# Norm in two steps between products, spread mixes, single-half tiles between full ones, and own bank and buffers at the end of a hybrid decoder step

## The chip, the cores and the metric

The kernel runs on one core of one Trainium2 chip. The metric is the device time of an execution in microseconds (us). TensorE (PE) multiplies, and its weight loads (PEld) overlap with that; VectorE (DVE) and ScalarE (ACT) do the elementwise work; SyncE (SP) issues DMAs in the order of its queue. The program is scheduled when it is built: each engine then has a fixed order of instructions, and semaphores hold an instruction until what it reads is there and what it overwrites is free.

## The reference, cut to what matters

One layer of a decoder for 1024 prompt rows and 8 sample rows (1032 in all, model width 1024). After sparse attention and a gated delta branch, merged by gates into `y`:

```python
x = x + merged @ w_out
hn = rms_norm(x, norm_ffn)
gg, uu = jnp.split(hn @ w_gate_up, 2, axis=-1)     # 1024 x (2 x 2816)
x = x + (jax.nn.silu(gg) * uu) @ w_down            # 2816 x 1024
```

The change touches only this last part: the product with `w_out`, the norm, the gate and up products, and the product with `w_down`.

## The kernel before, in words

Everything is held transposed: 128 model columns on partitions, the 1032 rows along the free axis. The rows form two halves of 516 (`HALF`), each of two quarters of 258 (`QT`). Every float32 factor is split into a high part (ACT, a copy in a rounded type, L187) and a low part (DVE, a difference, L188), and a product is three matmuls per 128 x 128 block: high by high, high by low, low by high (L163 to L165, L1706 to L1708).

`w45` is the last stage. `w_out(s)` makes the eight tiles of x for half s: per tile two products of 24 matmuls with 258 columns into the two buffers of `pj`, an evacuation of each on DVE (L1593, it adds the residual), a square on ACT and a running sum of squares `rs` on DVE (L1595, L1597).

`prepare(s)` is a generator that `w45` advances between other work. It multiplies the squares with ones on PE (L1608), takes the reciprocal root on DVE in ten tiny instructions (`nv`, `nr`, `nt`, L1610 and L196 to L200), transposes the result so that it lies along the free axis (L1616, PE), copies it to SBUF (L1617, ACT), and scales the eight tiles in place on DVE (L1620). Then it splits the blocks B11, B12, B21, B22 of the half, and the sums T1 to T4 of them (L1625), into high and low parts: tiles `hb` (and `b12`) with 1032 columns. For half 0 this runs beside `w_out(1)`, for half 1 beside the first gate and up tiles.

Gate and up have 22 tiles of 128 columns each. The plain form, `gate_up_plain`, does half 0 of the tiles 0 to 2 (`EARLY`), 192 matmuls each, while half 1 isn't ready; `e` counts gate and up in it, and `sg` holds the result. The other form, `gate_up`, is a seven-product scheme of Strassen's kind on quarters: differences of weight blocks are made on DVE (`mix`, L1683, into the scratch tile `rs`), and each of the seven products has 12 matmuls per half, 84 for one half and 168 for both. Its operands lie in seven buffers with the names `whi`, `wlo` and `wx`. The sums stand in four accumulator banks A, B, D, F, two buffers each. D takes the product with T1 first; DVE reads that to make `E` (L1729), then the product with B22 is added into the same bank, and DVE adds the result to `U`. After the plain tiles the single-half tiles 0 to 2 (half 1) come one after another, then tiles 3 to 20 for both halves, then tile 21 as two single halves. Weights come through two buffers `wraw` (L1678, L1679).

`down` multiplies with `w_down` in four groups of tiles. `load_act` reads an activation tile back from memory into a raw buffer (L1748) and splits it into `act`. The first and the second of these share one raw buffer, the start of `rs`. Results go out through `store_y`: transposes on PE (L1788), a copy to `yo` on ACT (L1790, two buffers for all three shapes in turn), and a DMA (L1792, L1794).

Of the kernel before, what the change touches and what calls it, by code (L numbers as in the profile page):

```python
# [9 lines left out]
F32 = mybir.dt.float32  # L10
# [10 lines left out]
T = 1032  # L21
# [33 lines left out]
class K:  # L55
# [1459 lines left out]
    def w45(self):  # L1515
        nc, I, O = self.nc, self.I, self.O
        op, end_o = self.pool("oa", side="right")
        xp, end_x = self.pool("x2")
        yp, end_y = self.pool("y")
        wk, end_wk = self.pool("stage")  # L1520
        rs = self.stage[:, 0:T]
        self.x2h.append(xp.tile([128, 4, T], F32, name="x21", bufs=1))
        x2 = lambda m: self.x2h[m // 4][:, m % 4]
        oa = self.oa = [[op.tile([128, T], F32R, name=f"oa{j}{x}", bufs=1) for x in range(2)] for j in range(4)]
        yhi = yp.tile([128, 8, T], F32R, name="yhi")
        ylo = yp.tile([128, 8, T], F32R, name="ylo")
        self.load_oa(oa, wk, 0, 3)
        weave(self.merge_a(oa, wk, yhi, ylo, 0, 2), PVS, self.sample, 4)
        for _ in self.merge_a(oa, wk, yhi, ylo, 2, 3):
            pass  # L1530
        self.x_T(1)
        end_wk()
        end_o()
        self.end_sa()
        self.nrm = xp
        h0, end_h0 = self.pool("h0", side="right")
        gf = xp.tile([128, 8], F32, name="gf")
        nc.sync.dma_start(gf, I['norm_ffn'][0].rearrange("(k p) -> p k", p=128))
        b12, end_b12 = self.pool("b12", side="right")
        H = [{}, {}]  # L1540
        for _ in self.w_out(0, (yhi, ylo), x2):
            pass
        prep = self.prepare(0, h0, H[0], gf, x2, b12)
        for m, _ in enumerate(self.w_out(1, (yhi, ylo), x2)):
            if m:
                next(prep, None)
        end_y()
        ex, end_ex = self.pool("gx")
        h1, end_h1 = self.pool("h1")
        self.end_pf()  # L1550
        self.end_ps()
        self.ps, end_ps = self.pool("psg", space=PSUM)
        self.pproj = lambda: self.ps.tile([128, 512], F32, name="A", tag="A", bufs=2)
        prep = self.prepare(1, h1, H[1], gf, x2)
        for f in range(EARLY):
            self.gate_up_plain(f, H[0], ex)
            for _ in islice(prep, 2 if f else 1):
                pass
        for _ in prep:
            pass  # L1560
        del self.pproj
        end_b12()
        self.wx, end_wx = self.pool("wx", side="right")
        for f in range(EARLY):
            self.gate_up(f, (1,), H, ex)
        for f in range(EARLY, 21):
            self.gate_up(f, (0, 1), H, ex)
            if f < EARLY + 4:
                nc.sync.dma_start(x2(f - EARLY), self.d_x2[f - EARLY])
        ops = self.gate_up(21, (1,), H, ex)  # L1570
        end_h1()
        a0, end_a0 = self.pool("act0")
        raws = [self.stage[:, 0:T], self.stage[:, 0:T], a0.tile([128, T], F32, name="araw", tag="araw", bufs=2)]
        first = [self.load_act(f, a0, 6, raws[f]) for f in range(3)]
        self.gate_up(21, (0,), H, ex, ops)
        end_ps()
        end_wx()
        end_h0()
        self.down(x2, a0, first)
        end_a0()  # L1580
        end_ex()
        end_x()
# [18 lines left out]
    def prepare(self, s, pool, H, gf, x2, b12=None):  # L1601

        nc = self.nc
        n = 86
        sqa = self.stage[:, HALF * (1 + s):HALF * (2 + s)]
        p = self.pproj()
        for j in range(6):
            nc.tensor.matmul(p[:n, j:j + 1], sqa[:, n * j:n * j + n], self.ones[:, 0:1], start=True, stop=True)  # L1608
        v, r, t = (self.nrm.tile([128, 6], F32, name=x, tag=x, bufs=1)[:n] for x in ("nv", "nr", "nt"))
        nc.vector.tensor_scalar(v, p[:n, 0:6], 1.0 / 1024, EPS, op0=ALU.mult, op1=ALU.add)  # L1610
        self.rsqrt(r, v, t=t)
        for c in range(2):
            p = self.pproj()
            for j in range(3):
                i = 3 * c + j
                nc.tensor.transpose(p[:, n * j:n * j + n], r[:, i:i + 1].to_broadcast([n, 128]), self.ident[:n, :n])  # L1616
            nc.scalar.activation(sqa[:, QT * c:QT * c + QT], p[:, 0:QT], AF.Copy)  # L1617
        for m in range(8):
            xv = x2(m)[:, HALF * s:HALF * s + HALF]
            nc.vector.scalar_tensor_tensor(xv, xv, gf[:, m:m + 1], sqa, op0=ALU.mult, op1=ALU.mult)  # L1620
        yield
        B11, B12, B21, B22 = (self.quarter(s, x) for x in ("B11", "B12", "B21", "B22"))

        def sub(name, dst, a, b):
            nc.vector.tensor_tensor(dst, a, b, op=ALU.subtract)  # L1625
            H[name] = self.block(pool, dst)
        H["B21"] = self.block(pool, B21)
        H["B11"] = self.block(pool, B11)
        yield
        if b12:  # L1630
            H["B12"] = self.block(b12, B12, "b12")
        H["B22"] = self.block(pool, B22)
        yield
        sub("T1", B11, B12, B11)
        sub("T3", B12, B22, B12)
        yield
        sub("T2", B22, B22, B11)
        sub("T4", B21, B21, B22)
        yield
# [9 lines left out]
        self.split(t[:, 0], t[:, 1], src)  # L1649
        return t  # L1650

    def gate_up_plain(self, f, H, ex):

        nc, gu = self.nc, self.I['w_gate_up'][0]
        sg = ex.tile([128, HALF], F32, name="sg", tag="sg", bufs=2)
        ws = [self.wcols(gu, 128 * f), self.wcols(gu, 2816 + 128 * f)]
        for e, (wh, wl) in enumerate(ws):
            for c in range(2):
                tag = "ABDF"[2 * e + c]
                p = self.ps.tile([128, 512], F32, name=tag, tag=tag, bufs=2)[:, :QT]  # L1660
                x1, x2 = H[f"B1{c + 1}"], H[f"B2{c + 1}"]
                self.mm3(p, [(wh[:, k], wl[:, k], x[:, 0, k % 4], x[:, 1, k % 4])
                             for k in range(8) for x in ((x1, x2)[k // 4],)])
                v = sg[:, QT * c:QT * c + QT]
                if e == 0:
                    nc.scalar.activation(v, p, AF.Silu)
                else:
                    nc.vector.tensor_tensor(v, v, p, op=ALU.mult)
        nc.sync.dma_start(self.d_act[f, :, 0:HALF], sg)

    def gate_up(self, f, halves, H, ex, ops=None):

# [21 lines left out]
            return t  # L1694
        U = {}
        st = self.x2h[1][:, 2 * (f % 2):2 * (f % 2) + 2]
        ps = {(t, s): self.ps.tile([128, 512], F32, name=t, tag=t, bufs=2)[:, :QT] for s in halves for t in "ABDF"}

        def product(src, x, t, first):
            a = operand(src)  # L1700
            made.append(a)
            for s in halves:
                b, p = H[s][x], ps[t, s]
                for k in range(4):
                    lh, ll, rh, rl = a[:, k], a[:, 4 + k], b[:, 0, k], b[:, 1, k]
                    nc.tensor.matmul(p, lh, rh, start=(first and k == 0), stop=False, skip_group_check=True)  # L1706
                    nc.tensor.matmul(p, lh, rl, start=False, stop=False, skip_group_check=True)  # L1707
                    nc.tensor.matmul(p, ll, rh, start=False, stop=(k == 3), skip_group_check=True)  # L1708
# [17 lines left out]
        for s in halves:  # L1726
# [1 line left out]
            e = part("E")  # L1728
            nc.vector.tensor_tensor(e, U[s], ps["D", s], op=ALU.add)  # L1729
            add(1, s, 1, e, ps["F", s])  # L1730
        product(lambda: mix(S[3], A12, S[2]), "B22", "D", False)
        for s in halves:
            add(0, s, 1, U[s], ps["D", s])
        product(lambda: A22, "T4", "F", False)
        for s in halves:
            t = slice(HALF * s, HALF * s + HALF)
# [43 lines left out]
    def store_y(self, m, x2, wk):  # L1780
        nc, O = self.nc, self.O
        cs = slice(128 * m, 128 * m + 128)
        for q in range(3):
            i0, ni, n = 4 * q, (4, 4, 1)[q], (128, 128, 8)[q]
            p = self.ptr()
            for j in range(ni):
                r0 = 128 * (i0 + j)
                nc.tensor.transpose(p[:n, j, :], x2(m)[:, r0:r0 + n], self.ident)  # L1788
            y = wk.tile([128, 4, 128], F32, name="yo", tag="yo", bufs=2)
            nc.scalar.activation(y[:n, :ni], p[:n, :ni], AF.Copy)  # L1790
            if q < 2:
                nc.sync.dma_start(O['y_p'][0, 512 * q:512 * q + 512, cs].rearrange("(i p) c -> p i c", p=128), y)  # L1792
            else:
                nc.sync.dma_start(O['y_s'][:, 0, cs], y[:8, 0])  # L1794
# [37 lines left out]
```

## Time and profile before

| what | value |
| --- | --- |
| median of three runs | 1805.31 us (1805.31, 1805.31, 1814.39) |
| profiled execution, its own time | 1802.74 us |
| span of its trace | 1801.0 us |
| PE busy | 1740.0 us, 97% of the span |
| weight loads busy | 1662.6 us |
| DVE busy | 1210.6 us, 67% |
| ACT busy | 852.1 us, 47% |
| mean granted clock | 0.995 |

The span runs from the first to the last instruction of the trace; the execution's own time is 1.7 us longer. Times in the rows are counted from the start of the span. A busy PE is not PE at its peak: matmuls overlap, so the number of matmuls in a stretch says more than its busy share. The stage of the change begins at about 1000 us and lasts to the end.

### The profile page before, as it was taken

The numbers are of one execution on the slowest core, as the hardware profiler recorded it, in microseconds if no ns is written. First come the engines' busy times: TensorE is split into PE (matmuls) and PEld (weight loads), VectorE is DVE, ScalarE is ACT, GpSimd is POOL, SyncE is SP. The second block draws the span as 40 slices with busy tenths as digits, with TensorE's granted clock in tenths as the row PEclk, the third lists the DMA queues.
The fourth block names the chain that finished last, engine by engine and source line by source line (L and its number), as shares of the span: only waits on it lengthen the run. The fifth ranks groups of instructions, "written<-read, shape, count | busy, mean of one in ns | idle before, by whom it ended". The sixth has DMA issues, their size and how long they took to land.

```text
span 1801.0 us, 31724 instructions
## 1 busy us (share of the span) xinstructions
PE 1740.0 (97%) x12276; PEld 1662.6 (92%) x12276; DVE 1210.6 (67%) x2776; ACT 852.1 (47%) x1575; POOL 42.2 (2%) x68
## 2 busy tenths in 40 slices
PE   5998999999999999999999999999999999999998
PEld 5998989999999988878899998999999999999998
DVE  7775558999899777797656477766666665733222
ACT  4567467877845345687444243433333333412012
POOL 3001100000000000000000000000000000000000
PEclk9999999999999999999999999999999999999999
DMA  6115434434546543254567434322222323732122
GB/s 194 43 35 153 130 101 145 130 113 120 159 131 167 149 137 109 84 183 141 195 235 226 138 110 135 101 81 85 82 72 75 91 72 125 223 100 73 51 80 69
DMA packets 293595, 218.01 MB, mean 121 GB/s; under 512 B 39292, under 2 KB 267456, under 8 KB 292412
## 3 DMA queue, kind: packets, MB, share of 16 engines
q1 hardware_dynamic: 291716, 205.50, 37.8%
q0 software_dynamic: 1728, 10.49, 1.7%
q8 instruction: 96, 1.57, 0.4%
q14 instruction: 55, 0.45, 0.1%
HBM read 154.17 MB, written 61.87 MB: 120 GB/s over the span
## 4 chain that ended last, share of the span: by engine, by line
PE 83%; DMA 7%; DVE 5%; ACT 3%; issue 2%; SPq 0%; ACTq 0%; DVEq 0%
PE pj L163 15%; PE pj L165 15%; PE pj L164 15%; PE A L1706 2%; PE A L1707 2%; PE A L1708 2%; PE D L1706 2%; PE F L1706 2%; PE F L1707 2%; PE D L1707 2%; PE F L1708 2%; PE D L1708 2%; PE PT L1055 1%; DMA araw<-d_act 1%; PE B L1706 1%
## 5 line engine op out<-in xcount | busy, mean ns | idle before, releaser
L163 PE MATMUL pj<-xhi,whi 128*128 128x344 f32 x912 | 297.5, 326 | 5.3 <-ACT gs L862 4.3
L165 PE MATMUL pj<-xhi,wlo 128*128 128x344 f32 x912 | 294.3, 323 | 0.0
L164 PE MATMUL pj<-xlo,whi 128*128 128x344 f32 x912 | 293.3, 322 | 0.0
L187 ACT ACTIVATE whi<-wraw 128x1024 fp32r<-128x1024 f32 (+4 forms) x126 | 115.2, 914 | 249.4 <-PE pj L164 208.0
L163 PEld LDWEIGHTS pj<-xhi,whi 128*128 128x128 f32 x912 | 171.9, 189 | 9.3 <-ACT gs L862 5.7
L164 PEld LDWEIGHTS pj<-xlo,whi 128*128 128x128 f32 x912 | 171.9, 188 | 2.0 <-issue 1.1
L165 PEld LDWEIGHTS pj<-xhi,wlo 128*128 128x128 f32 x912 | 171.9, 188 | 1.4
L164 PE MATMUL pj<-act,whi 128*128 128x344 f32 x528 | 170.3, 323 | 0.7 <-DVE act L188 0.7
L165 PE MATMUL pj<-act,wlo 128*128 128x344 f32 x528 | 168.9, 320 | 0.8 <-DVE wlo L188 0.8
L163 PE MATMUL pj<-act,whi 128*128 128x344 f32 x528 | 169.3, 322 | 0.2 <-DVE x L1768 0.2
L188 DVE TENSOR_TENSOR wlo<-wraw,whi 128x1024 fp32r<-128x1024 f32 (+3 forms) x104 | 116.2, 1118 | 54.4 <-ACT whi L187 52.7
L1768 DVE TENSOR_TENSOR x<-pj,x 128x344 f32<-128x344 f32 x96 | 48.5, 514 | 140.0 <-PE pj L165 139.9
L768 DVE TENSOR_SCALAR_CACHE_REDUCE kvb<-S,cand 128x384 bf16<-128x384 f32 (+3 forms) x128 | 103.7, 810 | 2.0
L165 PEld LDWEIGHTS pj<-act,wlo 128*128 128x128 f32 x528 | 99.2, 188 | 1.5 <-DVE wlo L188 1.3
L164 PEld LDWEIGHTS pj<-act,whi 128*128 128x128 f32 x528 | 99.2, 188 | 1.0 <-DVE act L188 1.0
L163 PEld LDWEIGHTS pj<-act,whi 128*128 128x128 f32 x528 | 99.2, 188 | 0.9 <-issue 0.4
L1706 PE MATMUL D<-hb,wx 128*128 128x258 f32 x328 | 93.0, 284 | 2.0 <-DVE E L1729 2.0
L1708 PE MATMUL D<-hb,wx 128*128 128x258 f32 x328 | 92.7, 282 | 0.7 <-DVE wx L188 0.7
L1706 PE MATMUL A<-hb,wlo 128*128 128x258 f32 x328 | 93.0, 283 | 0.0
L1707 PE MATMUL A<-hb,wlo 128*128 128x258 f32 x328 | 92.8, 283 | 0.0
L1708 PE MATMUL A<-hb,wlo 128*128 128x258 f32 x328 | 92.8, 283 | 0.0
L1707 PE MATMUL D<-hb,wx 128*128 128x258 f32 x328 | 92.6, 282 | 0.0
(587 smaller groups left out, 4790.3 us busy)
## 6 DMA issues: line engine op xcount, KB each, us to landing
wraw<-in_w_gate_up SPq DMA_DIRECT2D x50, 512.0 KB
wraw<-in_w_in SPq DMA_DIRECT2D x38, 512.0 KB
d_act<-x SPq DMA_DIRECT2D x41, 258.0 KB
araw<-d_act SPq DMA_DIRECT2D x20, 516.0 KB
d_g<-gs SPq DMA_DIRECT2D x48, 172.0 KB
wraw<-in_w_out SPq DMA_DIRECT2D x16, 512.0 KB
wraw<-in_w_branch SPq DMA_DIRECT2D x12, 512.0 KB
wraw<-in_w_down SPq DMA_DIRECT2D x16, 384.0 KB
```

Of the source, the lines that this page charges most:

```text
L163: nc.tensor.matmul(ps, lh, rh, start=(j == 0), stop=False)
L164: nc.tensor.matmul(ps, lh, rl, start=False, stop=False)
L165: nc.tensor.matmul(ps, ll, rh, start=False, stop=(j == last))
L187: self.nc.scalar.activation(hi, src, AF.Copy)
L188: self.nc.vector.tensor_tensor(lo, src, hi.bitcast(F32), op=ALU.subtract)
L768: nc.vector.tensor_scalar(junk[:r, :n], s, thr[:r, j:j + 1], 0.0, op0=ALU.is_lt, op1=ALU.add, accum_out=cnt[:r, j:j + 1])
L1055: nc.tensor.transpose(p[:, j, :], P[j][:, 128 * s:128 * s + 128], self.ident)
L1706: nc.tensor.matmul(p, lh, rh, start=(first and k == 0), stop=False, skip_group_check=True)
L1707: nc.tensor.matmul(p, lh, rl, start=False, stop=False, skip_group_check=True)
L1708: nc.tensor.matmul(p, ll, rh, start=False, stop=(k == 3), skip_group_check=True)
L1768: nc.vector.tensor_tensor(xv, p, xv, op=ALU.add)
```

## The change

- `prepare` yields once more, between the reciprocal root and the transposes.
- `gate_up_plain` is a generator too and yields after gate and after up; `prepare` for half 1 is advanced one step at each of these six points, where before it took two steps after tile 0, one after each of the tiles 1 and 2, and the rest at once.
- The single-half tiles 0, 1 and 2 come after the full tiles 3, 4 and 5, one each.
- In a `gate_up` for one half, the product with B22 goes into a second buffer of bank B, starts a sum of its own, and is added to `E` (which holds U + D) in place of `U`.
- `sg` is one tile with two halves, and the raw buffer of the second activation is this tile.
- The tiles `yo` for 4 and for 1 block have two buffers each.

```diff
@@ w45
-        for f in range(EARLY):
-            self.gate_up_plain(f, H[0], ex)
-            for _ in islice(prep, 2 if f else 1):
-                pass
-        for _ in prep:
-            pass
+        sg = ex.tile([128, 2, HALF], F32, name="sg", bufs=1)
+        for f in range(EARLY):
+            for _ in self.gate_up_plain(f, H[0], sg[:, f % 2]):
+                next(prep, None)
...
-        for f in range(EARLY):
-            self.gate_up(f, (1,), H, ex)
         for f in range(EARLY, 21):
             self.gate_up(f, (0, 1), H, ex)
+            if f < 2 * EARLY:
+                self.gate_up(f - EARLY, (1,), H, ex)
             if f < EARLY + 4:
                 nc.sync.dma_start(x2(f - EARLY), self.d_x2[f - EARLY])
...
-        raws = [self.stage[:, 0:T], self.stage[:, 0:T], a0.tile([128, T], F32, name="araw", tag="araw", bufs=2)]
+        raws = [self.stage[:, 0:T], sg.rearrange("p a b -> p (a b)"), a0.tile([128, T], F32, name="araw", tag="araw", bufs=2)]
@@ prepare
         self.rsqrt(r, v, t=t)
+        yield
         for c in range(2):
@@ gate_up_plain
-        nc.sync.dma_start(self.d_act[f, :, 0:HALF], sg)
+            if e == 1:
+                nc.sync.dma_start(self.d_act[f, :, 0:HALF], sg)
+            yield
@@ gate_up
+        one = len(halves) == 1
+        bank = lambda t: self.ps.tile([128, 512], F32, name=t, tag=t, bufs=2)[:, :QT]
...
-        product(lambda: mix(S[3], A12, S[2]), "B22", "D", False)
+        if one:
+            ps["D", s], U2 = bank("B"), e
+        product(lambda: mix(S[3], A12, S[2]), "B22", "D", one)
         for s in halves:
-            add(0, s, 1, U[s], ps["D", s])
+            add(0, s, 1, U2 if one else U[s], ps["D", s])
@@ store_y
-            y = wk.tile([128, 4, 128], F32, name="yo", tag="yo", bufs=2)
+            y = wk.tile([128, ni, 128], F32, name="yo", tag=f"yo{ni}", bufs=2)
```

How this moves instructions is seen in the order of the engines. First the first norm, beside `w_out(1)`. On DVE before, from the end of the reciprocal root on (`x_10114` and `x_10241` are the two tiles that hold x):

```order
L200 SCALAR_TENSOR_TENSOR nr<-nt,nr 86x6
L1620 SCALAR_TENSOR_TENSOR x_10114<-x_10114,gf,rs 128x516 x4
L1620 SCALAR_TENSOR_TENSOR x_10241<-x_10241,gf,rs 128x516 x4
L188 TENSOR_TENSOR b_11684<-x_10114,b_11684 128x1032
L1593 SCALAR_TENSOR_TENSOR x_10114<-pj,x_10114 128x258
L188 TENSOR_TENSOR hb<-x_10241,hb 128x1032
L1593 SCALAR_TENSOR_TENSOR x_10114<-pj,x_10114 128x258
```

and in the changed kernel:

```order
L200 SCALAR_TENSOR_TENSOR nr<-nt,nr 86x6
L1591 SCALAR_TENSOR_TENSOR x_10114<-pj,x_10114 128x258
L188 TENSOR_TENSOR wlo<-wraw,whi 128x1024
L1619 SCALAR_TENSOR_TENSOR x_10114<-x_10114,gf,rs 128x516 x4
L1619 SCALAR_TENSOR_TENSOR x_10241<-x_10241,gf,rs 128x516 x4
L1595 TENSOR_TENSOR rs<-rs 128x516
L1591 SCALAR_TENSOR_TENSOR x_10114<-pj,x_10114 128x258 x2
L188 TENSOR_TENSOR b_11745<-x_10114,b_11745 128x1032
```

The evacuations of the two products that were pulled ahead (L1591 here; the first of them a few rows further up) now stand before the scaling (L1619), together with a weight split; the next two come after the scaling and a sum of squares. On PE the two products, 48 matmuls, stand between the sums and the transposes. On ACT before:

```order
L1595 ACTIVATE rs<-x_10114 128x516
L187 ACTIVATE whi<-wraw 128x1024
L1595 ACTIVATE rs<-x_10114 128x516
L1617 ACTIVATE rs<-pj 128x258 x2
L187 ACTIVATE b_11684<-x_10114 128x1032
```

and now:

```order
L187 ACTIVATE whi<-wraw 128x1024
L1593 ACTIVATE rs<-x_10114 128x516
L187 ACTIVATE whi<-wraw 128x1024
L1616 ACTIVATE rs<-pj 128x258 x2
L1593 ACTIVATE rs<-x_10114 128x516
L187 ACTIVATE b_11745<-x_10114 128x1032
```

A weight split (`whi`) and the square of one of the products have moved to the two sides of the norm's copies. The second norm, beside the plain tiles: PE before, around the sums, and further on around the transposes, which stand 53 matmuls later:

```order
L165 MATMUL F<-hb,wlo 128x258
L1608 MATMUL A<-ones,rs 86x1 x6
L163 MATMUL B<-b_11684,whi 128x258
...
L164 MATMUL F<-b_11684,whi 128x258
L1616 MATMUL A<-ident,nr 128x86 x6
L165 MATMUL F<-b_11684,wlo 128x258
```

and now, where the sums stand after the gate half of tile 0, and the transposes 56 matmuls later:

```order
L165 MATMUL B<-hb,wlo 128x258
L1606 MATMUL A<-ones,rs 86x1 x6
L163 MATMUL D<-hb,whi 128x258
...
L164 MATMUL B<-b_11745,whi 128x258
L1615 MATMUL A<-ident,nr 128x86 x6
L165 MATMUL B<-b_11745,wlo 128x258
```

The sums have moved ahead by 48 matmuls, from behind the up half (F) of tile 0 to ahead of it (D, F), and with them the transposes. Last, the DMA queue: before, the second activation was read into `rs` among the last tiles,

```order
L1748 DMA araw<-d_act 128x1032 x2
L1740 DMA d_act<-x_10241 128x516
L1748 DMA rs<-d_act 128x1032
L139 DMA wraw<-in_w_down 128x3x128
L1748 DMA araw<-d_act 128x1032
```

and now it is read into `sg` among the weight loads behind the second single-half tile:

```order
L1744 DMA d_act<-x_10241 128x516
L1679 DMA wraw<-in_w_gate_up 128x8x128
L1752 DMA sg<-d_act 128x1032
L1678 DMA wraw<-in_w_gate_up 128x8x128
L1744 DMA d_act<-x_10241 128x516 x2
```

The load has moved ahead by some fifteen tiles.

## Rows read from the trace of the kernel before

**Rows 1.** Stretches: PE, PEld, DVE, ACT, POOL busy us (count), granted clock, DMA share, GB/s
```profile
1031.00:1040.00 9.00, 5.19 (x36) 5.11 (x36) 7.07 (x20) 2.59 (x5) 0.00 (x0) 0.81 0.27 88
...
1094.00:1150.00 56.00, 49.16 (x370) 46.51 (x369) 47.36 (x74) 26.20 (x43) 0.00 (x0) 0.97 0.42 132
...
1126.00:1136.00 10.00, 8.72 (x71) 8.30 (x69) 7.97 (x15) 4.47 (x9) 0.00 (x0) 1.00 0.34 97
...
1200.00:1500.00 300.00, 300.00 (x2499) 300.00 (x2498) 186.76 (x341) 102.90 (x195) 0.00 (x0) 1.00 0.26 79
```

**Rows 2.** PE's waits from 1000 us on: us in total, times, longest
```profile
PE pj L1616 <- DVE nr L200: 3.8, 1, 3.8
...
PE B L1706 <- ACT whi L187: 3.4, 2, 2.2
...
PE D L1706 <- DVE E L1729: 2.0, 2, 1.0
...
PE pj L165 <- DVE wlo L188: 0.8, 2, 0.5
...
PE pj L164 <- DVE act L188: 0.7, 1, 0.7
```

**Rows 3.** Timeline of PE at the first norm: start, us, what, [idle before <- releaser]
```profile
1030.65 1.01 PE L1608 MATMUL pj<-ones,rs 128*86 128x1 f32 x12
...
1035.46 0.66 PE L1616 MATMUL pj<-ident,nr 86*128 86x86 f32 x6 [3.81 <-DVE nr L200]
...
1036.19 0.42 PE L164 MATMUL pj<-ylo,whi 128*128 128x258 f32 x1
...
1039.42 0.30 PE L164 MATMUL pj<-ylo,whi 128*128 128x258 f32 x1
```

**Rows 4.** Timeline of DVE at the first norm
```profile
1031.87 1.23 DVE L188 TENSOR_TENSOR wlo<-wraw,whi 128x1024 fp32r<-128x1024 f32 x1
...
1033.08 0.68 DVE L1597 TENSOR_TENSOR rs<-rs 128x516 f32<-128x516 f32 x1
...
1036.63 5.42 DVE L1620 SCALAR_TENSOR_TENSOR x<-x,gf,rs 128x516 f32<-128x516 f32 x8 [1.22 <-ACT rs L1617]
...
1041.97 1.23 DVE L188 TENSOR_TENSOR b<-x,b 128x1032 fp32r<-128x1032 f32 x1
...
1043.12 0.42 DVE L1593 SCALAR_TENSOR_TENSOR x<-pj,x 128x258 f32<-128x258 f32 x1
```

**Rows 5.** Timeline of ACT: first norm, end of gate and up, last output
```profile
1024.98 1.06 ACT L187 ACTIVATE whi<-wraw 128x1024 fp32r<-128x1024 f32 x1 [4.15 <-PE pj L164]
...
1035.94 0.66 ACT L1617 ACTIVATE rs<-pj 128x258 f32<-128x258 f32 x2 [3.58 <-PE pj L1616]
...
1534.36 1.07 ACT L187 ACTIVATE act<-rs 128x1032 fp32r<-128x1032 f32 x1 [2.68 <-DMA rs<-d_act]
...
1798.28 0.27 ACT L1790 ACTIVATE yo<-tp 8x128 f32<-8x128 f32 x1 [1.75 <-DMA out_y_p<-yo]
```

**Rows 6.** Timeline of DVE: second norm, last block, a steady tile
```profile
1072.29 0.43 DVE L1593 SCALAR_TENSOR_TENSOR x<-pj,x 128x258 f32<-128x258 f32 x1 [2.23 <-PE pj L165]
...
1084.68 0.16 DVE L1610 TENSOR_SCALAR nv<-A 86x6 f32<-86x6 f32 x1 [0.35 <-PE A L1608]
...
1092.11 5.42 DVE L1620 SCALAR_TENSOR_TENSOR x<-x,gf,rs 128x516 f32<-128x516 f32 x8 [4.23 <-ACT rs L1617]
...
1121.07 1.22 DVE L188 TENSOR_TENSOR hb<-x,hb 128x1032 fp32r<-128x1032 f32 x1
...
1320.18 1.29 DVE L1683 TENSOR_TENSOR rs<-wraw 128x512 f32<-128x512 f32 x2 [0.65 <-DMA wraw<-in_w_gate_up]
```

**Rows 7.** Timeline of the DMA queue: a weight load, the last outputs
```profile
1315.84 0.38 SPq L1679 DMA_DIRECT2D wraw<-in_w_gate_up  x1
...
1795.84 1.09 SPq L1792 DMA_DIRECT2D out_y_p<-yo  x2
...
1798.57 0.30 SPq L1794 DMA_DIRECT2D out_y_s<-yo  x1
```

More of the change, by code (lines that the diff above doesn't have):

```diff
@@ L1650, in block, with gate_up_plain @@
         return t
-    def gate_up_plain(self, f, H, ex):
+    def gate_up_plain(self, f, H, sg):
         nc, gu = self.nc, self.I['w_gate_up'][0]
-        sg = ex.tile([128, HALF], F32, name="sg", tag="sg", bufs=2)
         ws = [self.wcols(gu, 128 * f), self.wcols(gu, 2816 + 128 * f)]
@@ L1696, in gate_up @@
         st = self.x2h[1][:, 2 * (f % 2):2 * (f % 2) + 2]
-        ps = {(t, s): self.ps.tile([128, 512], F32, name=t, tag=t, bufs=2)[:, :QT] for s in halves for t in "ABDF"}
+        one = len(halves) == 1
+        bank = lambda t: self.ps.tile([128, 512], F32, name=t, tag=t, bufs=2)[:, :QT]
+        ps = {(t, s): bank(t) for s in halves for t in "ABDF"}
         def product(src, x, t, first):
```

## Prediction

> **What bounds the kernel now.** I read the stretches of the run first, then PE's waits, then the timelines of PE, VectorE (DVE), ScalarE (ACT) and the DMA queue (SP) where PE waits. In the steady part of the gate and up products PE is busy all the time: 2499 matmuls in 300 us, 0.120 us each, at full granted clock, with DVE at 186.76 of 300 us [rows 1]. There nothing but fewer matmuls would help, and the change leaves the matmul count as it is. What it can win is the time in which PE stands or runs slowly, and that lies in four places.
>
> First norm (1031 to 1040). PE does the small matmuls of the sum, waits 3.81 us for DVE's reciprocal root, does six transposes, and then runs slowly: 15 matmuls from 1036.19 to 1039.42, 0.215 us apart [rows 3]. That is the lower of the two levels of the clock (1.2 GHz), after the long wait. 15 x (0.215 - 0.120) = 1.4 us; with the wait 5.2 us.
>
> Second norm, its blocks, and the three single-half tiles (1094 to 1150). PE does 370 matmuls where 56 us at the steady rate hold 466.5 [rows 1]. The 96.5 missing ones are 11.6 us. The waits name what is late: weights split by ACT 3.4 us, E on DVE about 1 of its 2.0 us, the rest in pieces [rows 2]; the clock's mean falls to 0.97 [rows 1].
>
> End of gate and up, start of down: 1.0 us for E, 0.7 for the second activation, 0.8 for weights, together 2.5 us [rows 2]. The very end: the last small output waits 1.75 us in ACT for an earlier store of the same buffer [rows 5].
>
> **First norm, in two steps.** The transposes move behind two whole products of w_out (48 matmuls, 5.8 us). The root comes 3.8 us after the sums, so this wait and its slow stretch go: -5.2 us. What is new stands in the order. On ACT a weight split (1.06 us) now stands ahead of the two copies of the norm (0.66 us together) [rows 5]; it waits for the same product as the transposes. Let t be the end of that product. Transposes are done at about t + 0.7 (the second group needs DVE's evacuation of that product, 0.43), the first copy at t + 1.4, and only then is the buffer of the next product free: PE stands 0.7 to 0.8 us. On DVE the low part of that weight (1.23) and the eight scalings (5.42) stand ahead of the evacuations; in a row each starts about 0.1 before the one ahead ends [rows 4]: scalings end at t + 1.1 + 1.1 + 5.4 = t + 7.6, the sum of squares takes 0.6, so the first evacuation ends at t + 8.5. The two products after the transposes end at t + 1.4 + 5.8 = t + 7.2, and the third needs that buffer: 1.3 us. New waits 2.1 us; the rest of w_out I walked through the same way, and there each evacuation comes 0.5 us or more ahead of its need. Bounds: 0, if copies and evacuations slip through, and 5.2, if the waits take all back. I take 2.1, since each piece has its row. Net -3.1.
>
> **Second norm, spread mixes, full tile first.** Count from the last evacuation of w_out at 1072.29 [rows 6], where PE starts the plain tiles. Before: the sums reach DVE at +12.4, because the norm begins after a whole plain tile; the scaling starts at +19.8, after 4.23 us of idle DVE, because the transposes stand 53 matmuls behind the sums; then DVE works with hardly a break until the last block is split at +50.0 [rows 6]. PE needs the plain tiles' 288 matmuls and the norm, 35.6 us, and then takes a single tile, of 12 matmuls (1.44 us) a product: the fifth product wants block T2 at +41.4, the last wants T4 at +44.2. Both are earlier than DVE can be. After: sums follow 48 matmuls (+5.8), transposes follow 56 more (+12.9), copies and a weight split 1.8 us, so the scaling starts at +14.7. With the same 30.2 us of DVE work behind it the last block is there at +44.9. The first tile is now a full one, 24 matmuls a product: T2 of the second half is wanted at 35.6 + 9 x 1.44 = +48.6, T4 at +54.3. Cover on both, 4 us or more.
>
> Then the singles. A full tile costs DVE 12.5 us (186.76/300 of 20.2 us). The operands, four differences and seven low parts at about 0.65 us [rows 6], are 7.1 of it and the same for a single; the additions halve. So a single asks 9.8 us of DVE for 10.1 us of PE, and a weight load of 4.34 us from issue (1315.84) to use (1320.18) [rows 6, 7] must fit between its last reader and the next tile. Three in a row leave nothing for it. With full ones between, a pair has 30.2 us of PE for 22.3 us of DVE. The own bank takes away the wait of the B22 product for E; it costs no matmul, since the partial sum is added from SBUF by the addition that stood there anyway. The four reloads of x2 and the stores of the plain tiles stay ahead of the first single's weights in SP; the first single now has a full tile's 20 us as cover. Of 11.6 us I keep 1.0, for a load that is late in the second or third pair, where I find the E additions only about 1 us ahead of PE. Bounds of what stays: 0, and 4.8 (in each of the three the wait of rows 2's second size, 3.4 - 2.2 = 1.2, and the small ones of 0.4). Net -10.6.
>
> **Own buffer for the second activation; own bank in tile 21.** Its load waited in the DMA queue for the split of the first one; ACT then waited 2.68 us for it [rows 5]. Now it is loaded into sg many tiles ahead. With the own bank, 1.0 + 0.7 go; of the 0.8 us for weights, behind a chain of loads that now starts earlier, I count half. Net -2.1, bounds 0 and -2.5.
>
> **Own buffer for the 8-row output.** ACT's last copy waits for a store; without it its DMA follows the previous issue, which ends at 1796.93, in place of 1798.57 [rows 7]. It landed 2.43 us after issue, which gives 1799.4 in place of 1801.0: -1.6, bounds 0 and -1.75.
>
> **Sum.** -3.1 - 10.6 - 2.1 - 1.6 = -17.4 us on the profiled 1802.74, 1785.3. The median of the runs shown, 1805.31, is 2.6 us above the profiled execution, so I forecast 1788 us.
>
> Now the clock, where a rule speaks against the change. After the wait of 3.81 us PE ran at the lower level; in the stretch 1126 to 1136, with PE idle for 1.28 us in all, the granted clock stayed at 1.00 [rows 1 to 3]. The Trainium skill, TensorE: Matmul & The Clock Gate, section "A second HAM failure mode: psum-queue depth-cycling", says that short idle spells between groups of matmuls, from cycling through accumulator banks, can make the clock swing between its levels. The rows side against it for waits near 1 us.
>
> **Rivals.**
> - Clock swings. Each of the two new waits in w_out is followed by a slow stretch like the one in rows 3: 2 x 1.4 = 2.8 us given back, 1791. That is what the rule just named would make of it.
> - The singles still wait: 4.8 us stay in place of 1.0, 1792. For: DVE takes its work in order, and the differences stand behind loads. Against: the pair's cover of 8 us.
> - w_out's evacuations behind DVE's block work cost all that the first norm gave (3.1 less gain), and the singles keep 4.8 (3.8 less): 1795. For: DVE has almost no idle from the scaling to the last block in w_out.
> - The change doesn't do what it says: the waits move from the first single to the first full tile, since DVE's 30 us of work are the same, and only the two last items win, 3.7 us: 1802.
> - Slower: after the two waits in w_out the clock doesn't come back before w_out ends. At 0.095 us a matmul the gain is gone after 17.4/0.095 = 183 matmuls, and 10 products are 240, 22.8 us: 1811. Against: it came back after 15 matmuls [rows 3].
>
> **How the numbers follow.** Forecast (1785 to 1791) 0.57, clock swings 0.08, singles wait 0.16, both evacuations and singles 0.10, waits only moved 0.06, slower 0.03. Half a per cent, 9 us, is about what a measurement can tell from no change. Below 1796.3 lie the first three and about half of the fourth: 0.85. Within: 0.12. Above 1814.3: 0.03, where the lower clock lasts into the plain tiles (278 matmuls or more). The range takes the bounds of all terms towards the fast side (-5.2 - 11.6 - 2.5 - 1.75 = -21.1, 1784; 3 us below that for what the walk leaves out) and reaches over the third rival, to 1798.
>
> **What would show it.** PE's wait of 3.8 us before the transposes is gone, and two of about 0.8 and 1.3 us stand in w_out, for the norm's copy and for an evacuation; the clock stays full there. DVE's second scaling starts about 15 us after the last evacuation of w_out. From the first full tile to the third single PE's rate is 8.33 matmuls a us. ACT's last copy has no DMA wait. I am wrong if PE waits in the first full tile for a block, if waits for weights behind loads come back in the singles, or if the clock falls in w_out.

## The result, and the profile after

| | before | after |
| --- | --- | --- |
| median of 7 runs each | 1807.01 us | 1787.12 us |
| profiled execution, its own time | 1802.74 us | 1784.55 us |
| span of its trace | 1801.0 us | 1782.7 us |

The ratio of the times is 0.9893, 95% interval [0.9862, 0.9924]: about 19 us less (14 to 25). The forecast was 1788 us, range 1781 to 1798.

Three statements ahead of this point are wrong. In this stage `pj` has five buffers, not two: the prediction's two new waits in `w_out` rest on the two. Before, `prepare` for half 1 was advanced one step after tile 0 and two steps after each of the tiles 1 and 2; the text on the change has these swapped. And a plain tile has 96 matmuls, not 192; the prediction's 288 for three of them is right. The times in the prediction were read from the trace and stand.

To see where the time went, I cut both traces at events that both have: PE's sums of the first norm, the first product of the plain tiles, SP's store of tile 20 (the last double store of `d_act<-x`), the first and the last product of `down`, the end of the span. That gives five stretches, which all later runs are read by:

| stretch | from, to | before | after | gain |
| --- | --- | --- | --- | --- |
| N | sums of the first norm, first plain product | 41.44 | 35.96 | 5.48 |
| G | to the store of tile 20 | 443.53 | 431.27 | 12.26 |
| D1 | to the first product of `down` (tile 21) | 19.66 | 20.12 | -0.46 |
| D2 | to the last product | 259.09 | 256.93 | 2.16 |
| Z | to the end of the span | 6.63 | 5.98 | 0.65 |

The sum is 20.1 us; the stretch ahead of N, in which the two programs are the same, took 1.8 us more in this trace of the change, and 18.3 us is left between the spans. N and G before, with the columns of [rows 1]:

```profile
1030.65:1072.09 41.44, 37.63 (x309) 37.55 (x308) 35.65 (x55) 18.37 (x22) 0.00 (x0) 0.96 0.36 115
1072.09:1515.62 443.53, 436.69 (x3600) 434.04 (x3599) 288.09 (x516) 160.42 (x292) 0.00 (x0) 1.00 0.29 88
```

Stretches of the changed kernel; the last two are N and G:

```profile
1031.00:1040.00 9.00, 9.00 (x84) 9.00 (x83) 4.61 (x16) 2.33 (x3) 0.00 (x0) 1.00 0.41 128
1104.00:1136.00 32.00, 32.00 (x268) 32.00 (x267) 24.37 (x45) 13.10 (x25) 0.00 (x0) 1.00 0.48 158
1200.00:1480.00 280.00, 280.00 (x2337) 280.00 (x2336) 176.14 (x322) 96.49 (x182) 0.00 (x0) 1.00 0.26 80
...
1032.44:1068.40 35.96, 35.96 (x308) 35.96 (x307) 32.67 (x53) 17.32 (x21) 0.00 (x0) 1.00 0.38 121
...
1068.40:1499.67 431.27, 431.27 (x3600) 431.27 (x3599) 289.08 (x519) 161.53 (x293) 0.00 (x0) 1.00 0.30 92
```

PE now does 84 matmuls where it did 36 from 1031 to 1040 [rows 1], at full clock. G holds 3600 matmuls, as before, but now 0.1198 us each, the steady rate from its first to its last product: here nothing is left but fewer matmuls. All of PE's waits from 1000 us on, to set against [rows 2]:

```profile
PE F L1708 <- DVE x L1714: 1.5, 1, 1.5
PE pj L165 <- DVE wlo L188: 0.3, 1, 0.3
```

The first norm on PE, on DVE and on ACT (beside [rows 3 to 5]); ACT's last row is the end of the kernel:

```profile
1032.44 1.01 PE L1606 MATMUL pj<-ones,rs 128*86 128x1 f32 x12
1039.12 0.61 PE L1615 MATMUL pj<-ident,nr 86*128 86x86 f32 x6
```

```profile
1041.48 5.42 DVE L1619 SCALAR_TENSOR_TENSOR x<-x,gf,rs 128x516 f32<-128x516 f32 x8
1046.82 0.69 DVE L1595 TENSOR_TENSOR rs<-rs 128x516 f32<-128x516 f32 x1
1047.42 0.75 DVE L1591 SCALAR_TENSOR_TENSOR x<-pj,x 128x258 f32<-128x258 f32 x2
```

```profile
1039.25 1.06 ACT L187 ACTIVATE whi<-wraw 128x1024 fp32r<-128x1024 f32 x1 [5.10 <-PE pj L164]
1040.21 0.65 ACT L1616 ACTIVATE rs<-pj 128x258 f32<-128x258 f32 x2
...
1777.57 1.46 ACT L1794 ACTIVATE yo<-tp 128x512 f32<-128x512 f32 x3 [4.94 <-PE tp L1792]
```

The transposes have no wait. The weight split stands ahead of the copies and the scalings ahead of the evacuations, as forecast; two evacuations come late, at 1047.42, and PE doesn't mind. The second norm on DVE (beside [rows 6]): last evacuation, sums, scaling, last block. The scaling starts 14.9 us after PE's first plain product (forecast 14.7), and the last block is split 41.5 us after it (forecast 44.9). The prediction counted from the last evacuation of `w_out`, which before came where the plain tiles start; now it comes 1.6 us later than that, so counted from it the scaling starts at 13.3.

```profile
1069.96 0.42 DVE L1591 SCALAR_TENSOR_TENSOR x<-pj,x 128x258 f32<-128x258 f32 x1
...
1075.22 0.16 DVE L1608 TENSOR_SCALAR nv<-A 86x6 f32<-86x6 f32 x1 [1.95 <-PE A L1606]
...
1083.26 5.42 DVE L1619 SCALAR_TENSOR_TENSOR x<-x,gf,rs 128x516 f32<-128x516 f32 x8
...
1108.70 1.23 DVE L188 TENSOR_TENSOR hb<-x,hb 128x1032 fp32r<-128x1032 f32 x1
```

The last DMAs (beside [rows 7]):

```profile
1778.19 1.09 SPq L1796 DMA_DIRECT2D out_y_p<-yo  x2
1779.37 0.39 SPq L1798 DMA_DIRECT2D out_y_s<-yo  x1
```

### The profile page after: what moved, and what is told of

Its sections match the earlier page's. It is cut to its first block, busy times and chain, and to the rows that moved or that the text cites. A ratio compares the mean times of both kernels' runs of the same rounds, so it can differ in the third digit from the quotient of the medians.

```text
span 1782.7 us, 31712 instructions
## 1 busy us (share of the span) xinstructions
PE 1736.5 (97%) x12276; PEld 1662.9 (93%) x12276; DVE 1207.6 (68%) x2776; ACT 852.3 (48%) x1575; POOL 42.6 (2%) x68
## 3 DMA queue, kind: packets, MB, share of 16 engines
q1 hardware_dynamic: 291716, 205.50, 38.1%
## 4 chain that ended last, share of the span: by engine, by line
PE 84%; DMA 5%; DVE 5%; issue 3%; ACT 2%; SPq 0%; POOL 0%; ACTq 0%; DVEq 0%; POOLq 0%
PE pj L163 15%; PE pj L165 15%; PE pj L164 15%; PE F L1708 2%; PE F L1710 2%; PE F L1709 2%; PE A L1708 2%; PE A L1709 2%; PE A L1710 2%; PE D L1708 2%; PE D L1710 2%; PE D L1709 2%; PE PT L1055 1%; PE B L1709 1%; PE B L1708 1%
## 5 line engine op out<-in xcount | busy, mean ns | idle before, releaser
L1708 PE MATMUL D<-hb,wx 128*128 128x258 f32 x308 | 87.1, 283 | 0.0
L1709 PE MATMUL D<-hb,wx 128*128 128x258 f32 x308 | 87.0, 282 | 0.0
L1710 PE MATMUL D<-hb,wx 128*128 128x258 f32 x308 | 87.0, 283 | 0.0
```

## The experiments

All runs by stretches (us); the row "again" of each kernel is an unaltered repeat. Ratios are to runs of the kernel before on the same chip; a run without one has a single execution, and its trace alone is used.

| run | N | G | D1 | D2 | Z | ratio |
| --- | --- | --- | --- | --- | --- | --- |
| before | 41.44 | 443.53 | 19.66 | 259.09 | 6.63 | 1 |
| before again (e11_before) | 41.79 | 443.55 | 19.66 | 258.18 | 6.63 | |
| change | 35.96 | 431.27 | 20.12 | 256.93 | 5.98 | 0.9893 [0.9862, 0.9924] |
| change again (e10_again) | 35.97 | 431.27 | 20.11 | 258.00 | 5.95 | |
| e1_norm | 35.97 | 443.85 | 19.65 | 258.15 | 6.92 | 0.9964 [0.9938, 0.9991] |
| e2_spread | 41.46 | 436.54 | 19.65 | 257.87 | 6.94 | 0.9926 [0.9897, 0.9955] |
| e3_order | 42.55 | 433.99 | 19.66 | 259.22 | 6.68 | 0.9909 [0.9875, 0.9943] |
| e4_nobank | 35.96 | 431.37 | 21.98 | 257.16 | 6.01 | 0.9867 [0.9822, 0.9911] |
| e5_pj2 | 40.59 | 431.26 | 20.11 | 257.04 | 6.03 | |
| e6_raw | 35.97 | 431.26 | 19.40 | 258.64 | 5.95 | |
| e7_yo | 35.96 | 431.27 | 20.12 | 258.97 | 6.68 | |
| e8_both | 35.97 | 431.26 | 20.12 | 258.25 | 5.51 | 0.9890 [0.9865, 0.9914] |
| e9_bank2 | 35.97 | 431.26 | 18.34 | 258.98 | 5.97 | 0.9897 [0.9867, 0.9926] |
| e12_raw3 | 35.96 | 431.27 | 18.34 | 258.13 | 5.96 | 0.9898 [0.9875, 0.9920] |

The times of one kernel spread by 10 us and more, so a part worth 2 us can't be seen in a ratio. N, G, D1 and Z come out within some tenths of a us again and again (N with the long wait within 1.1), and D2 within 1.1. Z is good to 0.05, as the spans are read to a tenth. Conclusions below go by these.

**The repeats** give that measure.

> The changed kernel unaltered, for how far its own stretches differ from run to run. Theory: N, G, D1 and Z come out within 0.3 us of 35.96, 431.27, 20.12 and 5.98; D2, where the activations' loads and splits run just ahead of TensorE, may move by 1 to 2 from 256.93; the stretch ahead of N by several us. Rival: D2 stays within 0.3, and the longer D2 of the runs with other buffers is due to their edits.

> The kernel before unaltered, for the same. Theory: N within 1.2 us of 41.44 (its clock is low behind a wait of 3.8, for a time that differs), G, D1 and Z within 0.4 of 443.53, 19.66 and 6.63, D2 within 1 of 259.09. Rival: G and N move by several us, and the ledger by stretches says less than it seems to.

The stretches did as the theories said, with 1.07 and 0.91 of difference in D2. One part missed: the stretch ahead of N moved by 1.0 in the repeat of the change, not by several us. So the 2.16 us that D2 seemed to give are not shown: in the two repeats it gives 0.18.

**e1_norm**: before, with the norm's new step for the first half alone.

```diff
-            for _ in islice(prep, 2 if f else 1):
+            for _ in islice(prep, 2):
...
         self.rsqrt(r, v, t=t)
+        yield
```

> The kernel before with the first half's norm alone in two steps. Four stretches of the trace are compared: N, from the norm's sums of the first half on TensorE to the first product of the plain tiles (41.44 us before, 35.96 in the change); G, from there to SyncE's store of tile 20's second half (443.53 and 431.27); D, from there to the last product (278.75 and 277.05); Z, from there to the span's end (6.63 and 5.98). Theory (pj has five buffers in w_out, so that a late evacuation holds up nothing): N is 36.0, the whole gain of 5.5; G, D and Z stay within 0.7 of before, and the time is some 5.5 us (0.3%) below before. Rival (the prediction's term: the idle time comes back in part as waits for a weight split and an evacuation, 2.1): N is 38.3. Rival (the clock stays low in w_out): N is above 40.

N is 35.97, all of the change's gain, and nothing is taken back. D missed "within 0.7" by 0.3, in D2.

**e5_pj2**: the change, with two buffers of `pj` for `w_out`, which is what the prediction had taken for granted.

```diff
         self.x_T(1)
+        self.end_pf()
+        self.pj_bufs = 2
+        self.pf, self.end_pf = self.pool("psw", space=PSUM)
```

> The changed kernel with the pool of pj opened again ahead of the first half's w_out, with two buffers in place of five. Stretches N, G, D, Z as in the first run's expectation. Theory (the prediction's two new waits of w_out, 0.8 for a weight split and 1.3 for an evacuation, stay away only since pj has five buffers): N grows from 35.96 us to 37 to 38.1, with a wait of TensorE for the evacuation at L1589 or L1591 behind the norm's transposes in the trace, and it may drop the clock. Rival (DVE is back in time, whatever the number of buffers): N stays within 0.3 of 35.96. G, D and Z as in the change.

Timeline of PE in N, its waits:

```profile
1042.94 0.44 PE L1618 MATMUL pj<-ident,nr 86*128 86x86 f32 x3 [0.29 <-DVE x L1594]
1043.77 0.39 PE L163 MATMUL pj<-yhi,whi 128*128 128x258 f32 x1 [0.40 <-ACT rs L1619]
...
1051.03 0.39 PE L163 MATMUL pj<-yhi,whi 128*128 128x258 f32 x1 [1.27 <-DVE x L1594]
...
1057.51 0.36 PE L163 MATMUL pj<-yhi,whi 128*128 128x258 f32 x1 [0.46 <-DVE x L1594]
```

Here are the prediction's waits: 0.29 and 0.40 for 0.7 to 0.8, and 1.27 for 1.3, at the products that it named. Then come more, which its walk had said would not come (0.46, and 0.71 at 1070.33), and N is 4.6 longer, beyond the theory's 38.1. So the arithmetic was right for a kernel with two buffers as far as the third product, and the kernel has five. The waits are followed by no slow stretch: the granted clock of N as a whole is 1.00.

```profile
1035.57:1076.16 40.59, 37.43 (x309) 36.27 (x307) 35.48 (x55) 18.43 (x22) 0.00 (x0) 1.00 0.36 116
```

The Trainium skill (TensorE: Matmul & The Clock Gate, section "A second HAM failure mode: psum-queue depth-cycling") speaks of a clock that swings when PE idles shortly and often between groups of matmuls. This trace shows no such swing behind five idle spells of 0.3 to 1.3 us, 0.8 to 12.8 us apart.

**e2_spread** and **e3_order**: before, with one of the two edits in G each. e2 advances `prepare` for half 1 as the change does and leaves the three single tiles in a row; e3 does the reverse.

```diff
# e3_order
-        for f in range(EARLY):
-            self.gate_up(f, (1,), H, ex)
         for f in range(EARLY, 21):
             self.gate_up(f, (0, 1), H, ex)
+            if f < 2 * EARLY:
+                self.gate_up(f - EARLY, (1,), H, ex)
```

> The kernel before with the second half's norm and mixes alone spread over the plain tiles (one step behind each of their six pairs of products); three single halves in a row, as before. Stretches N, G, D, Z as in the first run's expectation. Theory (both the late blocks and the three singles in a row cost time, and the singles more, since each wants a weight load and seven splits per 10 us): G falls from 443.5 to 437 to 439, half of the change's 12.3. Rival (the late blocks are all of it): G is 431 to 433. Rival (only the order of the tiles matters): G stays above 442. N, D and Z as before.

> The kernel before with the single halves of tiles 0 to 2 alone moved behind the full tiles 3 to 5; the norm and the mixes of the second half stand as before. Stretches as in the first run's expectation. Theory (the singles in a row cost more than the late blocks): G falls from 443.5 to 434 to 437. Rival (the blocks of the second half are what is late, and a full tile needs them as soon as a single does): G stays above 440. N, D and Z as before.

e2 gains 7.0 us of G, e3 9.5, the change with both 12.3. Each theory is right in kind, and e2 gains a little more than it said. The gains overlap by 4.3 us. A reading of that, which no run tests, is that either edit alone already gives DVE slack that the other would give. What e2 keeps (timeline of PE, two of its five waits there) are the singles' waits, for E and for each single's first weights:

```profile
1115.28 0.39 PE L1707 MATMUL D<-hb,wx 128*128 128x258 f32 x1 [0.94 <-DVE E L1730]
1117.77 0.39 PE L1707 MATMUL B<-hb,whi 128*128 128x258 f32 x1 [0.78 <-ACT whi L187]
```

and e3 keeps waits for weights in the plain tiles, just behind the scaling of the second half's norm:

```profile
1101.72 0.39 PE L163 MATMUL D<-hb,whi 128*128 128x258 f32 x1 [0.55 <-ACT whi L187]
...
1102.92 0.39 PE L165 MATMUL A<-hb,wlo 128*128 128x258 f32 x1 [0.46 <-DVE wlo L188]
```

**e4_nobank**: the change without the single halves' own bank.

```diff
-        if one:
-            ps["D", s], U2 = bank("B"), e
-        product(lambda: mix(S[3], A12, S[2]), "B22", "D", one)
+        product(lambda: mix(S[3], A12, S[2]), "B22", "D", False)
         for s in halves:
-            add(0, s, 1, U2 if one else U[s], ps["D", s])
+            add(0, s, 1, U[s], ps["D", s])
```

> The changed kernel without the single halves' own bank and sum (D and U as before). Theory (the prediction's: without it each single half waits about 0.9 us for the evacuation to E, as the trace of before shows twice): G is 2.5 to 3 longer than in the change (433.8 to 434.3), with TensorE's waits for DVE E at L1731 back, and D is up to 1 longer (277 to 278). Rival (between full tiles DVE has the time, and the evacuation is in time): G stays within 0.5 of 431.3, and the time is that of the change.

The theory falls for G, 431.37: between full tiles E is in time without a bank of its own. It pays in tile 21 alone, where D1 grows by 1.9. There ACT and DVE split an activation (1517.80 and 1519.26 in the chain of work) ahead of E (1520.49). Timeline of PE, then stretches:

```profile
1517.08 0.28 PE L1708 MATMUL A<-hb,wlo 128*128 128x258 f32 x1
...
1520.87 0.39 PE L1708 MATMUL D<-hb,wx 128*128 128x258 f32 x1 [2.18 <-DVE E L1731]
```

```profile
1508.40:1518.50 10.10, 10.10 (x86) 10.07 (x84) 5.57 (x9) 5.19 (x8) 0.00 (x0) 1.00 0.62 215
...
1521.00:1524.50 3.50, 3.50 (x22) 3.50 (x23) 0.70 (x2) 0.63 (x1) 0.00 (x0) 0.69 0.54 176
```

After this wait of 2.18 us the clock is low for a while (granted 0.69 in that stretch), as after the 3.8 us of [rows 3]. After the change's 1.5 us in the same place it is not:

```profile
1518.20:1522.00 3.80, 3.76 (x27) 3.77 (x28) 2.22 (x4) 2.65 (x3) 0.00 (x0) 1.00 0.36 125
```

**e6_raw**: the change with the first two activations loaded into one buffer again (the second entry of `raws` is `self.stage[:, 0:T]`).

> The changed kernel with the first two activations of the last projection loaded into one buffer again, one after the other. Stretches as in the first run's expectation. Theory (the prediction's: the second load then waits for the first one's split, some 2.7 us, and group 0 for it): D grows from 277.05 us to 278 to 279. Rival (the split that comes later leaves DVE free for the sums of tile 21, so that TensorE's wait of 1.5 us for DVE x at L1714 goes as well): D stays at 276.5 to 277.5.

D is 278.04, where the theory had it, and that tells nothing, since the unaltered repeat has 278.11. What is shown is a shift: D1 is 0.7 shorter, and PE's wait there 0.8 in place of 1.5 (why, is told at e8).

**e7_yo**: the change with one tag of two `yo` buffers again.

> The changed kernel with one tag of two output buffers for all three stores of a column block, as before. Stretches as in the first run's expectation. Theory (the trace of the change: its last 8-row store lands 3.3 us from its issue behind two stores of 256 KB): Z grows from 5.98 us to 6.6, as in the two runs with the old buffers (6.63 to 6.94). Rival (the prediction's term of 1.6): Z is 7.5.

Z is 6.68: the buffers are worth 0.7, not 1.6. D2 has a wait of 1.6 us of PE in group 1, though the order of instructions on every engine is that of the change; there DVE stands behind an activation that came late (timeline of DVE):

```profile
1548.52 1.23 DVE L188 TENSOR_TENSOR act<-araw,act 128x1032 fp32r<-128x1032 f32 x1 [2.32 <-ACT act L187]
```

**e8_both**: the change with two edits to win back the 1.5 us wait and more of the end.

```diff
-        raws = [self.stage[:, 0:T], sg.rearrange("p a b -> p (a b)"), a0.tile([128, T], F32, name="araw", tag="araw", bufs=2)]
+        raws = [self.stage[:, 0:T], sg.rearrange("p a b -> p (a b)"), self.stage[:, 0:T]]
...
@@ down
-                self.proj_T(self.wcols(dn[128 * f0:128 * f1], 128 * m, f1 - f0), act, evac)
+                    if last and t1 in (512, T):
+                        self.store_y(m, x2, wk, (0,) if t1 < T else (1, 2))
+                last = gi == 3 and m == 7
+                self.proj_T(self.wcols(dn[128 * f0:128 * f1], 128 * m, f1 - f0), act, evac, 0, T, (0, 512, 772, T) if last else None)
...
```

> The changed kernel with two edits more. First, the third activation is loaded into the buffer of the first, so that its split stands on DVE behind the sums of tile 21 in place of ahead of them. Second, the last column block is cut at tokens 512 and 772 in place of 344 and 688, and its first 512 tokens are transposed and stored while TensorE works on the others. Stretches as in the first run's expectation. Theory: TensorE's wait of 1.5 us for DVE x at L1714 goes, so D falls from 277.05 us to 275.5 to 276; the end holds one copy and one store of 256 KB less (0.6 and 0.9), so Z falls from 5.98 to 4.4 to 4.8; the time is 2.4 to 3.1 us below that of the change. Rival (the third activation comes too late for group 0): D is 277 or more, with a wait of TensorE for the split at L188. Rival (what ends the kernel is the time from issue to landing, not the bytes): Z is above 5.5.

Both parts of the theory fall. The third split did move behind the sums, and the wait is still 1.50, so the splits were not its cause. Z is 5.51 and no better than the rival: the first 512 columns are transposed only 1.6 us ahead of the last product (1780.86 and 1782.49), and the four transposes now stand in D2.

That leaves the chain itself. In the change's tile 21 (timelines of PE, ACT and DVE), the B22 product, which with its own bank hangs on nothing, is put ahead of the fifth product, the one with T2 into A (the next expectation calls it the third). So when A is done nothing but F is left, and F waits for U, E and the sum that reads F's first product:

```profile
1513.70 0.29 PE L1708 MATMUL B<-hb,wx 128*128 128x258 f32 x1
1515.13 0.28 PE L1708 MATMUL A<-hb,wlo 128*128 128x258 f32 x1
1518.24 0.39 PE L1708 MATMUL F<-hb,wx 128*128 128x258 f32 x1 [1.50 <-DVE x L1714]
```

```profile
1516.78 0.39 ACT L1719 ACTIVATE U<-A 128x258 f32<-128x258 f32 x1 [2.35 <-PE A L1710]
```

```profile
1517.31 0.42 DVE L1731 TENSOR_TENSOR E<-U,D 128x258 f32<-128x258 f32 x1
1517.76 0.42 DVE L1714 TENSOR_TENSOR x<-E,F 128x258 f32<-128x258 f32 x1
```

In e6 six of the B22 product's twelve matmuls stood behind A, and the wait was 0.8.

**e9_bank2**: the change, with a bank of its own for that last product too (in the last single half).

```diff
             ps["D", s], U2 = bank("B"), e
+            if ops:
+                nc.vector.tensor_tensor(U[s], U[s], ps["F", s], op=ALU.add)
+                ps["F", s] = bank("F")
...
-        product(lambda: A22, "T4", "F", False)
+        product(lambda: A22, "T4", "F", bool(ops))
```

> The changed kernel with one edit: in the last single half (tile 21, first half) the last product too has a bank of its own, and U takes up F's first product in one more addition of DVE, so that no product there waits for the chain U, E, sum that the change's trace shows ahead of it (1.5 us). D is taken in two parts: D1, from the store of tile 20's second half to the first product of the last projection (19.66 us before, 20.12 in the change), and D2, from there to the last product (259.09 and 256.93). Theory (the mixed product, which has its own bank, is put ahead of the third product, so nothing is left to cover the chain): D1 falls by the 1.5 to 18.6 or 18.7, D2 stays at 257 to 259, the time falls by some 1.5. Rival (the first activations' splits, which stand on DVE among the sums, are what is late): TensorE waits as long at the first product of the last projection, and D1 and D2 together stay at 277 or more. N, G and Z as in the change.

The wait is gone and D1 is 18.34, 1.8 less: the chain was its cause. But D1 and D2 together are 277.3, as the rival had it, though not in its place: PE loses the time over the first 40 us of `down`. In D2's first 50 us PE does 317 matmuls in the change, 310 in its repeat, 304 in e9, and afterwards all run alike. There SP's loads stand behind splits that must free a buffer (waits of e9's DMA queue, 1520 to 1575):

```profile
SPq L1755 <- DVE act L188: 27.0, 14, 3.2
```

That window begins 7 us ahead of e9's D2. Over D2's first 50 us it is 24.0 us, and 24.2 and 24.8 in the two runs of the change, so these waits alone don't tell why e9 does fewer matmuls there.

**e12_raw3**: e9 with three buffers to load activations into (the third entry of `raws` has three as well).

```diff
-                act = [self.load_act(f, pool, bufs, a0.tile([128, T], F32, name="araw", tag="araw", bufs=2))
+                act = [self.load_act(f, pool, bufs, a0.tile([128, T], F32, name="araw", tag="araw", bufs=3))
```

> The kernel with the second own bank (e9_bank2) and, for the last projection's activations, three buffers to load into in place of two. In the traces of the two kernels and of e9_bank2 the first 50 us of the last projection hold all of what differs in D2; there SyncE's loads of activations wait 24 to 27 us in all for DVE's splits to free one of the two buffers. Theory (that chain of load, split, load paces TensorE there, so that a group that starts earlier only waits later): D1 is 18.3 as in e9_bank2 and D2 falls to 256 to 257, D1 and D2 together 274.3 to 275.5 against 277.05 and 278.11 in the two runs of the change; the time is some 2 to 3 us below the change's. Rival (the loads come at some 200 to 255 GB/s there and can come no faster): D2 stays at 258 to 259, D1 and D2 together at 276.5 or more. N, G and Z as in the change.

D is 276.47: 0.6 and 1.6 below the two runs of the change, not the 2 to 3 of the theory, and at the rival's edge; D2 is 258.13, where the rival had it. The loads' waits for a free buffer over D2's first 50 us fell from 24.0 (e9) to 18.0 us. The rival's reason doesn't hold either: DMA moved 263 to 289 GB/s in the first 30 us of D2, against 204 to 255 in the two runs of the change. Now a weight load is late instead (waits of ACT in `down`):

```profile
ACT whi L187 <- DMA wraw<-in_w_down: 8.0, 2, 6.1
```

What sets the pace there stays open.

By its stretches this is the shortest version (the sum from the norm's sums to the end is 749.7 us; the change 750.3 and 751.3), and by its ratio nothing sets it apart from the change.

## Why the prediction came out right

The forecast sum was -17.4 us. By the stretches, and with D taken over the traces named below, it was about -19, with two terms too small and two too large. The total came nearer than its parts: terms that were 4.1 us too small stand against terms that were 2.3 us or more too large, and that these offset in part is luck.

- **First norm, net -3.1: it was -5.5.** The wait and its slow stretch went (5.2 forecast). The new waits, 2.1, failed on their premise: the evacuations are as late as worked out, but `pj` has five buffers. e5 shows the forecast waits when there are two, and e1 that the step alone gives all.
- **Second norm, spread, order: -10.6: it was -12.3.** The scaling came within 0.2 us of its date and the last block 3.4 us ahead of it, the singles have no wait, and the 1.0 us kept back wasn't needed. The rest lies outside the 56 us that were counted. Of the two causes that it named, which overlap, three singles in a row is the larger (e3) and the late blocks the smaller (e2); the own bank, which was to take away E's wait in the singles, has no part in G (e4). The prediction gave the mean clock of 0.97 no part of its own. In the trace of before, the low part of that mean stands behind PE's wait of 2.2 us for a single's weights, with 19 matmuls where 3.5 us at the steady rate hold 29:

```profile
1121.30:1124.80 3.50, 3.50 (x19) 3.50 (x18) 2.09 (x4) 0.39 (x1) 0.00 (x0) 0.51 1.02 365
```

So some 1.2 of the 11.6 us were the clock's, and they went with that wait.

- **Second activation and bank in tile 21, -2.1: not shown, some 0.3 to 0.7.** Of the traces whose order in D is as before, five have a D (D1 and D2) of 277.5 to 278.9 with a mean of 278.2; the change, its repeat and e5 have 277.1 to 278.1 with a mean of 277.4. With e7, alike but for `yo` and at 279.1, the mean of the four is 277.9. Either difference is less than the 1.1 by which one kernel's D2 moves. ACT's wait for the load and PE's for E are gone, and a new one of 1.5 us for x stands in tile 21, which the prediction had not looked for: it asked what the bank removes, not what comes next once the bank frees a product to move.
- **Last output, -1.6: it was -0.7.** ACT's wait for the DMA went, and the small store is issued 2.65 us after the last product in place of 4.20, 1.55 earlier, as forecast. But it landed 3.3 us after its issue, not 2.43. That number was taken from a store that was issued when the two big ones ahead of it were nearly through; now they are in full flow, at 240 GB/s until 1781.2:

```profile
1779.00:1781.20 2.20, 0.00 (x0) 0.00 (x0) 0.00 (x0) 0.03 (x1) 0.00 (x0) 1.00 0.82 240
1781.20:1782.70 1.50, 0.00 (x0) 0.00 (x0) 0.00 (x0) 0.00 (x0) 0.00 (x0) 0.66 0.00 0
```

The Trainium skill (DMA: Bandwidth & Descriptors, section "Queues, rings and completion order") says that each DMA engine takes the descriptors of a ring in order. The trace fits it: the small store was issued last, its bytes moved within the flow of the two big ones, which ends by 1781.2, and the span ends 1.5 us later. It doesn't tell the packets of the three apart. With the 0.9 us more that this took (3.33 - 2.43), the term's 1.55 comes to 0.7.

Of the rivals, "clock swings" and "slower" fell with the new waits; e5 has such waits and no slow stretch. "The singles still wait" and "waits only moved" are refuted by G, in which PE never stops, and the rival that joined late evacuations with waiting singles by N and G together.

## What to carry to other kernels

Before an evacuation's delay is priced, count the buffers at that stage: a late evacuation is free until the ring of buffers comes round (no wait with five here, five waits with two). When a dependence is taken away, ask where the freed instruction goes: here the build-time scheduler put it early, and what it used to cover stood bare. And when a wait of 1 to 2 us is removed, look at the sum with the next stretch: in e9 the 1.8 us that D1 gained did not show in D1 and D2 together. Whether the next stretch took them back or its own spread of 1.1 us hides a part, one trace can't tell.

## What the runs showed that I had not expected

The part of the program ahead of N, which is the same in all these kernels but for the place of a few transposes in e5, ended anywhere from 1028.6 us (e2) to 1041.9 us (e9): 13 us, more than most of the parts under study. Part of it is the clock. From 600 to 700 us e2's trace has

```profile
600.00:700.00 100.00, 98.15 (x645) 88.51 (x644) 73.83 (x234) 45.40 (x83) 0.00 (x0) 1.00 0.40 118
```

and e9's

```profile
600.00:700.00 100.00, 97.26 (x605) 88.86 (x604) 69.31 (x228) 41.63 (x82) 0.00 (x0) 0.91 0.41 117
```

with 40 matmuls less at a granted clock of 0.91. What makes the clock fall there in one run and not in another, the traces don't tell. It is why N, G, D1 and Z, which repeat to a few tenths, can settle parts that no ratio of whole times can.
